# Fifty-one element-wise instructions of a Fourier-mixer encoder layer moved from GpSimd to VectorE

## The chip, the cores and the metric

The kernel runs on one core of a Trainium2 chip. The core has TensorE (PE in the profile, matmuls), VectorE (DVE), ScalarE (ACT), GpSimd (POOL) and SyncE (SP, whose queue issues most of the transfers here). The metric is the time of one execution on the device in microseconds, as a median over runs. Less is better.

## The reference

One layer of a bidirectional encoder on x of shape 1024 x 1024 (positions x channels), float32, with a conditioning vector c. Cut to what is computed (only layer 0 runs, since DEPTH is 1):

```python
mod = silu(c) @ ada_w + ada_b
sh1, sc1, g1, sh2, sc2, g2 = split(mod, 6)
h = layer_norm(x) * (1 + sc1) + sh1
y = real(fft2(h in 8 groups of 128 channels, over positions and channels)) @ w_out
x = layer_norm(ALPHA * x + g1 * y) * ln_mix_g + ln_mix_b
h = layer_norm(x) * (1 + sc2) + sh2
u = h @ w_up                                   # 1024 -> 2 x 2816
u = depthwise conv of width 3 over positions(u) + conv_b
y = (gelu(gate) * val) @ w_down                # 2816 -> 1024
x = layer_norm(ALPHA * x + g2 * y) * ln_ffn_g + ln_ffn_b
```

## The kernel before

Nearly all matmuls work on numbers split into two parts of a shorter float format: `split(hi, lo, src)` has ScalarE copy `src` to `hi` and VectorE (or another engine that is named) subtract `hi` from `src` to give `lo`. Each product is then three matmuls, high x high, high x low and low x high (`hl3`, lines 284 to 286). So every operand costs a ScalarE copy and an element-wise subtraction before TensorE can use it.

The stages in order of time are these.

- Norm and folds (to about 54 us). x is normalised in eight row tiles; tiles are paired, and for each half of the channels (c0 = 0 and 512) sums and differences of pairs are formed: `fb` and `bw` (differences, the odd products), `s` (sums, written over x), `fe` (sums and differences of the sums, the even products). `fold_split` forms a fold and splits it; its low parts are `b`, `bhl` and `el`. `c1_split` splits the three DFT tables into `c1h` and `c1l`.
- Odd and even products `po` and `pe` (the DFT over positions), scaled into `uh` and `ul`, then the DFT over channels in `pp` and `pq`, split into `P` and `Q`. Between them lie the matmuls `ada` of the modulation vectors, whose weights `aw` are loaded through few buffers.
- Mixer weights. `w_prep` loads two tiles per group of channels and GpSimd forms their sum and difference `we` and `wa`. After the gate row `g1` is broadcast, each of the eight is multiplied by `g1` (line 358) and split into `wh` and `wl`.
- Output of the mixer, `A` and `B`, over four pairs of row tiles, with residual, norm, modulation and transposes into `h2t`. GpSimd makes the inverse deviation (`pow`) and some normalised tiles `hm`.
- Up projection. `h2t` is split into `Hh` and `Hl` in four groups of positions; the first two tiles j = 0 and 1 of w_up are used plainly (`plain_w`, parts `a`); `comb` forms the position combinations T1 to T4, which are split into TT1 to TT4; from j = 2 on each tile is done with seven products in place of eight, for which GpSimd forms S1 to S4 of the weights (lines 633 to 636).
- Down projection with the second norm, from about 615 us.

`E(name)` gives GpSimd if the name stands in `ON_POOL`, else VectorE. The order of the instructions in each engine's queue is laid down when the program is built: a planner (`TileContext(..., schedule_with_timeline_sim=True)`) goes through them with costs of its own and issues on each engine what it takes to be ready, in the order of the program where several are. So an instruction given to another engine changes the order of others too. On the chip each queue runs in that order.

Of the kernel before, what the change touches and what calls it, by code (L numbers as in the profile page):

```python
# [11 lines left out]
ALU = mybir.AluOpType  # L12
# [10 lines left out]


ON_POOL = frozenset((
    "H0", "H1", "T1", "T2", "T4", "a0", "a1", "c1l0", "c1l1", "c1l2", "fb0_0", "fb0_512", "fb1_0", "fe00_512",
    "lb1_512", "lb2_512", "lb3_512", "le00_0", "le10_512", "s0_512", "s2_0", "s3_512", "ve2",
))

IN_NAMES = (  # L30
# [6 lines left out]
def encoder_layer(ctx: ExitStack, tc: tile.TileContext, I, out: bass.AP):  # L37
    nc = tc.nc
    act, dve, pool, pe, sp = nc.scalar, nc.vector, nc.gpsimd, nc.tensor, nc.sync
# [6 lines left out]
    def slot(i, shape, dt, name):  # L46
        return big.tile([128] + list(shape), dt, tag=f"s{i}", name=name)
# [4 lines left out]
    def split(hi, lo, src, eng=None):  # L52
        act.activation(hi, src, AF.Copy)  # L53
        (eng or dve).tensor_tensor(lo, src, hi, ALU.subtract)  # L54
# [40 lines left out]
    def bank(i, name, shape=(512,)):  # L95
        return ps.tile([128] + list(shape), F32, tag=f"b{i}", name=name)
# [12 lines left out]
    def ada_load(sec, part=0, parts=1):  # L109

        n = 1024 // parts
        abt = cp.tile([128, 256], F32, tag="abt", bufs=2, name=f"abt{sec}_{part}")
        sp.dma_start(abt[:, : n // 4], I["ada_b"][sec] if parts == 1 else I["ada_b2"][sec, part])
        ws = []
        c0 = 1024 * sec + n * part
        for i in range(KT // parts):
            sl = AW[sec]
            w = slot(sl[(i if sec == 4 else n_aw[0]) % len(sl)], [parts, n], F32, f"aw{sec}_{part}_{i}")
            n_aw[0] += 1
            rows = I["ada_w"][128 * parts * i : 128 * parts * (i + 1), c0 : c0 + n]  # L120
            sp.dma_start(w, rows.rearrange("(k p) n -> p k n", p=128))
            ws += [w[:, k, :] for k in range(parts)]
        return abt, ws, n // 4, f"{sec}_{part}"
# [5 lines left out]
    def ada_mm(sec, loaded, col=None, bk=7, plus=0.0, c0=0, kts=range(KT)):  # L129
        abt, ws, q, nm = loaded  # L130
        if kts[0] == 0:
            pms[sec] = bank(bk, f"ada{nm}", (q,))
        pm = pms[sec]
        for kt in kts:
            for g in range(4):
                pe.matmul(pm[32 * g : 32 * g + 32, :], cb[:, kt, :], ws[kt][:, q * g : q * g + q],
                          start=(kt == 0), stop=(kt == KT - 1), tile_position=(0, 32 * g))
        if kts[-1] != KT - 1:
            return
        if col is not None:  # L140
            act.activation(abt[:, :q], pm, AF.Copy)
        else:
            dve.tensor_tensor(abt[:, :q], pm, abt[:, :q], ALU.add)
        mod_r[sec] = abt
        if col is not None:
            nb_ = q // 128
            pt = bank(7, f"adat{nm}", (nb_, 128))
            for b in range(nb_):
                pe.transpose(pt[:, b, :], abt[:, 128 * b : 128 * b + 128], ident)
            dst, src = col.rearrange("p (i b) -> p i b", b=nb_), pt.rearrange("p b (i r) -> p i b r", r=32)[:, :, :, 0]  # L150
            bias = adab[:, sec, c0 : c0 + 4 * nb_].rearrange("p (i b) -> p i b", b=nb_)
            dve.scalar_tensor_tensor(dst, src, plus, bias, ALU.add, ALU.add)

    def row_bcast(sec, dst, get_bank, scale=1.0):
        for h in range(2):
            pb = get_bank(f"bc{sec}_{h}")
            for q in range(2):
                pe.matmul(pb[:, 256 * q : 256 * q + 256], sel[:, 2 * h + q, :], mod_r[sec], start=True, stop=True)
            act.activation(dst[:, 512 * h : 512 * h + 512], pb, AF.Copy, scale=scale)
# [109 lines left out]
    g1 = slot(7, [D], F32, "g1")  # L269
# [13 lines left out]
    def hl3(ps_ap, hi_l, lo_l, hi_r, lo_r, first, last):  # L283
        pe.matmul(ps_ap, hi_l, hi_r, start=first, stop=False)  # L284
        pe.matmul(ps_ap, hi_l, lo_r, start=False, stop=False)  # L285
        pe.matmul(ps_ap, lo_l, hi_r, start=False, stop=last)  # L286
# [5 lines left out]
    def mm_odd(c):  # L292
        c0 = c // 4 * 512
        cs = slice(128 * c - c0, 128 * c - c0 + 128)
        po = obank(f"po{c}")
        for i, t in enumerate((0, 2, 1, 3)):
            if c0 not in bh[t]:
                pe.matmul(po, bw[t][:, cs], stage_c1[t // 2][:, t % 2, :], start=(i == 0), stop=(i == 3))
                continue
            hl3(po, bh[t][c0][:, cs], bl[t][c0][:, cs], c1h[t // 2][:, t % 2, :], c1l[t // 2][:, t % 2, :], i == 0, i == 3)  # L300
        return po

    def mm_even(c):
        cs = slice(128 * c, 128 * c + 128)
        pv = obank(f"pe{c}")
        for q in range(2):
            fs = slice(256 * q, 256 * q + 256)
            for t in range(2):
                hl3(pv[:, fs], eh[q][t][:, cs], el[q][t][:, cs], c1h[2][:, t, fs], c1l[2][:, t, fs], t == 0, t == 1)
        return pv  # L310

    def odd(u):
        return u.rearrange("p (h i r) -> p h i r", h=2, r=2)[:, :, :, 1]

    def even(u):
        return u.rearrange("p (h i r) -> p r h i", h=2, r=4)[:, 0:4:2]
# [4 lines left out]
    for c in range(8):  # L321
        pv = mm_even(c)
        po = pos_.pop(c)
        uh = slot(2 * (c % 3), [1024], F32R, f"uh{c}")
        ul = slot(2 * (c % 3) + 1, [1024], F32R, f"ul{c}")
        po_v = po.rearrange("p (h i) -> p h i", h=2)
        pv_v = pv.rearrange("p (q h i) -> p q h i", q=2, h=2)
        sc = sc1[:, c : c + 1]
        act.activation(odd(uh), po_v, AF.Identity, scale=sc)
        dve.scalar_tensor_tensor(odd(ul), po_v, sc, odd(uh), ALU.mult, ALU.subtract)  # L330
        last_u = act.activation(even(uh), pv_v, AF.Identity, scale=sc)
        dve.scalar_tensor_tensor(even(ul), pv_v, sc, even(uh), ALU.mult, ALU.subtract)
        dve.tensor_scalar(dcs[:, c, :], pv[:, 0:256:128], sc, None, ALU.mult)
        uv[c] = (uh, ul)
        if c + LOOK < 8:
            pos_[c + LOOK] = mm_odd(c + LOOK)
        for k, u in enumerate((uh, ul)):
            pe.matmul(pN, nyt[:, c, :], u[:, 0:512], start=(c == 0 and k == 0), stop=(c == 7 and k == 1))
        if c % 2 == 0:
            continue  # L340
        gp = c // 2
        pp = bank(4, f"pp{gp}")
        pq = bank(5, f"pq{gp}")
        for dst, base, rng in ((pp, 0, slice(0, 512)), (pq, 256, slice(512, 1024))):
            for e in range(2):
                uh, ul = uv[2 * gp + e]
                ls = slice(base + 128 * e, base + 128 * e + 128)
                hl3(dst, dch_h[:, ls], dch_l[:, ls], uh[:, rng], ul[:, rng], e == 0, e == 1)
        P_t[gp] = slot(36 + gp, [2, 512], F32R, f"P{gp}")
        Q_t[gp] = slot(40 + gp, [2, 512], F32R, f"Q{gp}")  # L350
        split(P_t[gp][:, 0, :], P_t[gp][:, 1, :], pp)
        pool.memset(Q_t[gp][:, :, 0:1].bitcast(F32), 0.0)
        split(Q_t[gp][:, 0, 1:512], Q_t[gp][:, 1, 1:512], pq[:, 1:512])
        if c == 1:
            row_bcast(G1, g1, lambda n: bank(4 + int(n[-1]), n), 1.0 / ALPHA)
            for gp in range(4):
                for w in w_raw[gp]:
                    pool.tensor_tensor(w, w, g1, ALU.mult)
        if c == 1:
            ada_mm(SH1, ada_load(SH1), sh1)  # L360
            shpm = cp.tile([128, 8, 2], F32, name="shpm")
            for k, sgn in ((0, 1.0), (1, -1.0)):
                dve.tensor_scalar(shpm[:, :, k], sh1, sgn * HALF_DC, None, ALU.mult)
        if c == 3:
            sh2 = cp.tile([128, 8], F32, name="sh2")
            ada_mm(SH2, ada_load(SH2), sh2)
        if c == 5:
            sc2 = cp.tile([128, 8], F32, name="sc2")
            ada_mm(SC2, ada_load(SC2), sc2, plus=1.0)
# [201 lines left out]
    a0 = plain_w(0, (45, 44, 31, 32))  # L571
# [30 lines left out]
    a1 = plain_w(1, (33, 24, 25, 26))  # L602
    T1 = comb("T1", B[0, 1], B[0, 0], ALU.subtract, 34)
    T2 = comb("T2", B[1, 1], T1, ALU.subtract, 46)
# [3 lines left out]
    T4 = comb("T4", T2, B[1, 0], ALU.subtract, 31)  # L608
# [317 lines left out]
    for n, (p, i) in enumerate(steps):  # L926
# [51 lines left out]
        for m in range(4):  # L978
            ms = slice(128 * m, 128 * m + 128)
            w = 512 // len(acc[m])  # L980
# [112 lines left out]
```

## Time and profile before

| | |
|---|---|
| time, median of 3 runs | 866.1 us (865.58 to 866.92) |
| the profiled execution's own time | 866.72 us |
| its span, first to last instruction | 864.9 us |
| TensorE busy | 799.9 us, 92% |
| VectorE busy | 708.3 us, 82% |
| ScalarE busy | 387.3 us, 45% |
| GpSimd busy | 328.9 us, 38% |
| mean granted clock of TensorE | 0.974 |

The profile is one execution of the kernel. A busy share is a mean over stages with different limits; which engine waits for which, and when, is read from the views of waits, of stages and of the timeline.

### The profile page before, as it was taken

To read this page: it belongs to the slowest core of one execution; us is meant where nothing else is said; L and a number is where in the kernel's file an instruction comes from. 1 tells how busy PE (TensorE), PEld (TensorE's weight loads), DVE (VectorE), ACT (ScalarE), POOL (GpSimd) and SP (SyncE) were. 2 spreads that over 40 slices of the span, in tenths; PEclk is the share of its full clock that TensorE was granted. 3 is DMA by queue.
4 is the path that set the end of the run, shared out by engine and by line. 5 is a ranking of instruction groups with operands and counts; after the bars stand their busy time and mean duration, and the time that the engine had idled before them with its cause. 6 is when DMAs were issued, how large, how long until landed. Compare 5 with 4: busy or idle time off the path is not lost.

```text
span 864.9 us, 10742 instructions
## 1 busy us (share of the span) xinstructions
PE 799.9 (92%) x3943; PEld 644.2 (74%) x3943; DVE 708.3 (82%) x979; ACT 387.3 (45%) x559; POOL 328.9 (38%) x256
## 2 busy tenths in 40 slices
PE   2699799997979999999999999999999989999990
PEld 1466577776868888888888888888887868888880
DVE  6972857899899999998888888888677784556897
ACT  7442514676454344444444444444444324335611
POOL 5767802498355434334334333431000112702203
PEclk9899899999989999999999999999999999999995
DMA  9759665562113222322212222210498887988903
GB/s 342 260 181 309 248 230 210 186 262 74 49 49 97 98 74 74 111 84 98 74 73 74 87 90 92 98 50 25 156 375 309 264 215 147 190 157 240 294 26 122
DMA packets 50613, 133.90 MB, mean 155 GB/s; under 512 B 5608, under 2 KB 6760, under 8 KB 50560
## 3 DMA queue, kind: packets, MB, share of 16 engines
q1 hardware_dynamic: 39504, 103.59, 34.1%
q0 software_dynamic: 10768, 28.58, 13.4%
q10 hardware_dynamic: 288, 1.05, 0.3%
q8 instruction: 31, 0.51, 0.2%
q14 instruction: 22, 0.18, 0.1%
HBM read 110.39 MB, written 19.92 MB: 151 GB/s over the span
## 4 chain that ended last, share of the span: by engine, by line
PE 57%; DVE 6%; DMA 6%; issue 2%; POOL 1%; ACT 1%; SPq 0%; POOLq 0%; ACTq 0%; DVEq 0%
PE x L286 14%; PE x L284 14%; PE x L285 14%; PE o L285 5%; PE o L286 5%; PE o L284 5%; DMA gr<-gd 2%; DMA xu<-x1d 2%; DMA wd<-in_w_down_dram 1%; DVE d_1l L54 1%; DVE d_0l L54 1%; DMA Sg<-gd 1%; DVE C L864 1%; POOL S L635 0%; DVE C L894 0%
## 5 line engine op out<-in xcount | busy, mean ns | idle before, releaser
L285 PE MATMUL x<-Hl,a 128*128 128x512 f32 (+2 forms) x416 | 156.7, 378 | 4.8 <-DVE Hl L54 4.0
L284 PE MATMUL x<-Hh,a 128*128 128x512 f32 (+2 forms) x416 | 155.6, 377 | 4.6 <-ACT a L53 4.6
L286 PE MATMUL x<-Hh,a 128*128 128x512 f32 (+2 forms) x416 | 155.9, 375 | 0.0
L285 PE MATMUL o<-d_1l,d_0h 128*128 128x512 f32 (+1 forms) x299 | 115.0, 386 | 4.0 <-DVE d_1l L54 4.0
L286 PE MATMUL o<-d_1h,d_0l 128*128 128x512 f32 (+1 forms) x299 | 114.4, 384 | 0.0
L284 PE MATMUL o<-d_1h,d_0h 128*128 128x512 f32 (+1 forms) x299 | 102.8, 383 | 0.0
L285 PEld LDWEIGHTS x<-Hl,a 128*128 128x128 f32 x416 | 79.0, 190 | 20.2 <-DVE Hl L54 5.1
L284 PEld LDWEIGHTS x<-Hh,a 128*128 128x128 f32 x416 | 78.5, 190 | 20.8 <-ACT a L53 5.5
L53 ACT ACTIVATE a<-S 128x512 fp32r<-128x512 f32 x80 | 50.4, 630 | 96.2 <-PE x L286 87.9
L286 PEld LDWEIGHTS x<-Hh,a 128*128 128x128 f32 x416 | 79.0, 190 | 14.6 <-POOL nbm L478 0.4
L588 POOL DMA_DIRECT2D gd<-ug x20 | 11.4, 568 | 170.2 <-DVE ug L587 170.2
L285 PEld LDWEIGHTS o<-d_1l,d_0h 128*128 128x128 f32 x299 | 56.8, 190 | 16.5 <-DVE d_1l L54 5.3
L54 DVE TENSOR_TENSOR a<-wu,a 128x512 fp32r<-128x512 f32 x60 | 63.5, 1059 | 3.0 <-ACT a L53 3.0
L286 PEld LDWEIGHTS o<-d_1h,d_0l 128*128 128x128 f32 x299 | 56.6, 189 | 10.9
L284 PEld LDWEIGHTS o<-d_1h,d_0h 128*128 128x128 f32 x299 | 56.2, 188 | 11.0
L54 DVE TENSOR_TENSOR a<-S,a 128x512 fp32r<-128x512 f32 x80 | 60.9, 762 | 0.8
L635 POOL TENSOR_TENSOR S<-wu 128x512 f32<-128x512 f32 x20 | 29.9, 1493 | 69.1 <-DVE a L54 60.4
L53 ACT ACTIVATE a<-wu 128x512 fp32r<-128x512 f32 x60 | 37.5, 626 | 40.5 <-PE x L286 38.6
L733 POOL DMA_DIRECT2D Sg<-gd x12 | 14.7, 1266 | 89.3 <-DVE d_0l L54 89.3
L579 DVE SCALAR_TENSOR_TENSOR t<-uv,cw,t 128x1023 f32<-128x1023 f32 x20 | 35.9, 1793 | 11.4 <-ACT t L578 11.3
L54 DVE TENSOR_TENSOR d_1l<-wd,d_1h 128x1024 fp32r<-128x1024 f32 (+1 forms) x37 | 44.0, 1189 | 0.0
L636 POOL TENSOR_TENSOR S<-wu,S 128x512 f32<-128x512 f32 x20 | 43.9, 2195 | 0.1
(325 smaller groups left out, 1929.7 us busy)
## 6 DMA issues: line engine op xcount, KB each, us to landing
aw<-in_ada_w_dram SPq DMA_DIRECT2D x48, 512.0 KB, 6.0
wu<-in_w_up_dram SPq DMA_DIRECT2D x44, 512.0 KB, 3.2
gd<-ug POOLq DMA_DIRECT2D x20, 512.0 KB, 2.9
wd<-in_w_down_dram SPq DMA_DIRECT2D x20, 512.0 KB, 9.7
gr<-gd SPq DMA_DIRECT2D x15, 512.0 KB, 7.4
gA<-gd SPq DMA_DIRECT2D x10, 512.0 KB, 10.7
Sg<-gd POOLq DMA_DIRECT2D x10, 512.0 KB, 6.5
x<-in_x_dram SPq DMA_DIRECT2D x8, 512.0 KB, 5.4
```

What stands on the lines that cost most here:

```text
L53: act.activation(hi, src, AF.Copy)
L54: (eng or dve).tensor_tensor(lo, src, hi, ALU.subtract)
L284: pe.matmul(ps_ap, hi_l, hi_r, start=first, stop=False)
L285: pe.matmul(ps_ap, hi_l, lo_r, start=False, stop=False)
L286: pe.matmul(ps_ap, lo_l, hi_r, start=False, stop=last)
L579: dve.scalar_tensor_tensor(tt[:, 1:S], u[:, 0 : S - 1], w[:, 0:1], tt[:, 1:S], ALU.mult, ALU.add)
L588: pool.dma_start(gd[j], gg)
L635: pool.tensor_tensor(S3, A11, A21, ALU.subtract)
L636: pool.tensor_tensor(S4, A12, S2, ALU.subtract)
L733: pool.dma_start(raw_g[p, i] if p == 7 else Sg[i], gd[k0 : k0 + n, :, 512 * mh : 512 * mh + 512].rearrange("k p c -> p k c"), accum_op=ALU ...
L864: dve.scalar_tensor_tensor(c1[:, lo], c1[:, lo], rs, ffb[:, lo], ALU.mult, ALU.add)
```

## The change

The names in `ON_POOL` are taken out, all but `ve2`, and the eight gate products are given to VectorE. Moved from GpSimd to VectorE are thus: three low parts `c1l` (128x1024); twelve folds, sums and low parts of folds (128x512); eight gate products (128x1024); the low parts of groups 0 and 1 of the up projection's input for every second tile, eight of 128x256; the low parts of the first two up tiles, eight of 128x512; the combinations T1, T2 and T4, twelve of 128x512. That is 51 instructions. GpSimd keeps `pow`, `nbm`, `hm`, the sums and differences `we` and `wa`, S1 to S4, its memsets and its transfers.

```diff
 ON_POOL = frozenset((
-    "H0", "H1", "T1", "T2", "T4", "a0", "a1", "c1l0", "c1l1", "c1l2", "fb0_0", "fb0_512", "fb1_0", "fe00_512",
-    "lb1_512", "lb2_512", "lb3_512", "le00_0", "le10_512", "s0_512", "s2_0", "s3_512", "ve2",
+    "ve2",
 ))
@@
             for gp in range(4):
                 for w in w_raw[gp]:
-                    pool.tensor_tensor(w, w, g1, ALU.mult)
+                    dve.tensor_tensor(w, w, g1, ALU.mult)
```

## Rows read from the trace of the kernel before

**Rows 1.** The first part of the page: the span, and for each engine its busy microseconds, share of the span and instructions.
```profile
span 864.9 us, 10742 instructions
...
PE 799.9 (92%) x3943; PEld 644.2 (74%) x3943; DVE 708.3 (82%) x979; ACT 387.3 (45%) x559; POOL 328.9 (38%) x256
```

**Rows 2.** The table of stages: start and end of the stretch and its length in us, then for each engine its busy us and the number of its instructions, the granted clock of TensorE (1.00 is full speed), the mean busy share of the DMA engines, and GB/s.
```profile
15.00:45.00 30.00, 20.85 (x156) 12.65 (x156) 29.16 (x34) 15.39 (x24) 22.86 (x14) 0.89 0.80 282
...
60.00:95.00 35.00, 35.00 (x260) 23.66 (x260) 15.11 (x19) 15.53 (x21) 28.53 (x14) 1.00 0.86 290
...
172.00:200.00 28.00, 24.77 (x211) 19.20 (x209) 26.13 (x65) 20.63 (x52) 25.03 (x26) 1.00 0.63 236
200.00:230.00 30.00, 27.09 (x151) 23.64 (x152) 30.00 (x33) 15.12 (x34) 21.25 (x14) 0.94 0.10 36
...
265.00:615.00 350.00, 350.00 (x1546) 289.97 (x1545) 315.97 (x394) 152.78 (x205) 126.81 (x90) 1.00 0.22 80
```

**Rows 3.** The view of the waits of TensorE up to 270 us: line and tile of the waiting matmul, what it waited for, and the total in us, the number of times and the longest.
```profile
PE po L286 <- DVE b L54: 5.6, 1, 5.6
PE x L284 <- ACT a L53: 4.6, 2, 2.5
PE B L285 <- DVE wl L54: 4.6, 2, 2.3
PE x L285 <- DVE Hl L54: 4.0, 4, 1.8
PE pe L286 <- DVE el L54: 1.3, 1, 1.3
PE po L284 <- DVE ul L330: 1.1, 1, 1.1
```

**Rows 4.** The same table as rows 2 for short stretches.
```profile
80.00:90.00 10.00, 10.00 (x73) 5.90 (x73) 4.02 (x7) 4.79 (x7) 10.00 (x5) 1.00 0.91 311
30.00:35.00 5.00, 1.18 (x3) 0.99 (x4) 4.97 (x7) 2.06 (x4) 2.81 (x2) 0.63 1.03 403
35.00:40.00 5.00, 4.39 (x16) 3.34 (x14) 5.00 (x5) 2.66 (x8) 3.69 (x3) 0.69 0.13 42
100.00:105.00 5.00, 3.24 (x8) 2.56 (x9) 5.00 (x8) 2.07 (x2) 4.00 (x3) 0.50 0.49 190
210.00:215.00 5.00, 3.21 (x15) 2.98 (x15) 5.00 (x6) 2.87 (x8) 5.00 (x4) 0.72 0.18 70
```

**Rows 5.** The timeline of VectorE around 25 to 31 us: start and duration in us, engine, line, operation, output and inputs by the names of the program, shapes, and count.
```profile
25.63 1.77 DVE L54 TENSOR_TENSOR el<-fe,eh 128x512 fp32r<-128x512 f32 x1
...
30.20 0.69 DVE L246 TENSOR_TENSOR x<-x,x 128x512 f32<-128x512 f32 x1
30.81 0.68 DVE L198 TENSOR_TENSOR fb<-x,x 128x512 f32<-128x512 f32 x1
```

**Rows 6.** The timeline of GpSimd in the same stretch, columns as before.
```profile
25.12 1.73 POOL L54 TENSOR_TENSOR el<-fe,eh 128x512 fp32r<-128x512 f32 x1
```

**Rows 7.** The timeline of VectorE at three instructions that give prices: a 128x1024 product, a 128x256 subtraction, and the instruction behind it.
```profile
116.60 1.22 DVE L388 TENSOR_TENSOR wnr<-wnr,g 128x1024 f32<-128x1024 f32 x1 [3.49 <-DMA wnr<-in_w_ny_dram]
...
172.30 0.41 DVE L54 TENSOR_TENSOR Hl<-h2t,Hh 128x256 fp32r<-128x256 f32 x1
172.63 0.68 DVE L455 SCALAR_TENSOR_TENSOR s<-B,xr 128x512 f32<-128x512 f32 x1
```

**Rows 8.** The groups of VectorE instructions from 14.6 to 54 us, one line of the kernel and one shape to a group: busy us in total and mean ns of one, then the idle time before them.
```profile
L198 DVE TENSOR_TENSOR fe<-x,x 128x512 f32<-128x512 f32 x7 | 10.2, 1497 | 0.0
L246 DVE TENSOR_TENSOR x<-x,x 128x512 f32<-128x512 f32 x5 | 6.6, 1335 | 0.1
L54 DVE TENSOR_TENSOR el<-fe,eh 128x512 fp32r<-128x512 f32 x6 | 6.2, 1040 | 0.0
L198 DVE TENSOR_TENSOR fb<-x,x 128x512 f32<-128x512 f32 x4 | 5.8, 1462 | 0.0
...
L54 DVE TENSOR_TENSOR bhl<-fb,bhl 128x512 fp32r<-128x512 f32 x1 | 1.8, 1772 | 0.0
```

**Rows 9.** The timeline of GpSimd over the gate products, first and last of eight (the last line holds two).
```profile
81.17 2.38 POOL L358 TENSOR_TENSOR we<-we,g 128x1024 f32<-128x1024 f32 x1
...
97.27 6.69 POOL L358 TENSOR_TENSOR wa<-wa,g 128x1024 f32<-128x1024 f32 x2
```

**Rows 10.** The timeline of ScalarE where the gate row g1 is written.
```profile
77.55 0.60 ACT L159 ACTIVATE g<-bc 128x512 f32<-128x512 f32 x1 [0.27 <-PE bc L158]
```

**Rows 11.** The groups of VectorE instructions from 78 to 112 us, columns as in rows 8.
```profile
L54 DVE TENSOR_TENSOR wl<-wa,wh 128x1024 fp32r<-128x1024 f32 x4 | 9.1, 2312 | 0.0
L54 DVE TENSOR_TENSOR wl<-we,wh 128x1024 fp32r<-128x1024 f32 x4 | 7.5, 1916 | 2.5 <-ACT wh L53 2.5
```

**Rows 12.** The groups of VectorE instructions from 168 to 227 us, columns as in rows 8.
```profile
L54 DVE TENSOR_TENSOR Hl<-h2t,Hh 128x256 fp32r<-128x256 f32 x16 | 9.3, 610 | 0.0
L54 DVE TENSOR_TENSOR Hl<-h2t,Hh 128x258 fp32r<-128x258 f32 x8 | 9.1, 1173 | 0.0
...
L54 DVE TENSOR_TENSOR TT1l<-T,TT1h 128x512 fp32r<-128x512 f32 x4 | 6.0, 1500 | 0.0
L54 DVE TENSOR_TENSOR TT2l<-T,TT2h 128x512 fp32r<-128x512 f32 x4 | 4.8, 1225 | 0.0
...
L537 DVE TENSOR_TENSOR T<-h2t,h2t 128x512 f32<-128x512 f32 x4 | 4.8, 1229 | 0.0
```

## Prediction

> **What bounds the kernel now.** I read the page first: TensorE (PE) is busy 92% of the 864.9 us span [rows 1]. That is a mean over stages, so the next view is the table of stages [rows 2]. From 265 to 615 us PE is busy all 350 us; nothing that the change touches lies there, and what is gained in front of it only moves it. From 60 to 95 us PE is also never idle. It is idle from 15 to 45 us (20.9 of 30 us busy) and from 172 to 230 us (24.8 of 28, 27.1 of 30). The view of PE's waits names the causes [rows 3]: 5.6, 1.3 and 1.1 us for low parts b, el and ul that VectorE (DVE) writes in the stage of the odd and even products; 4.6 us for wl, the low parts of the mixer weights; 4.0 us for Hl, the low parts of the up projection's input; 4.6 us for a, a high part written by ScalarE.
>
> After three of these waits PE runs slower as well. In 30 to 40, 100 to 105 and 210 to 215 us the mean granted clock is 0.50 to 0.72, a mix of the two levels 1.2 and 2.4 GHz [rows 4]. Busy time times the missing share of the clock is what that costs: 1.18 x 0.37 + 4.39 x 0.31 = 1.8 us, 3.24 x 0.50 = 1.6 us, and 3.21 x 0.28 = 0.9 us.
>
> DVE feeds PE in these stages, and DVE is full there: 29.2 of 30 us from 15 to 45 us, 26.1 of 28 and 30.0 of 30 us from 172 to 230 us [rows 2]. What is in those busy microseconds decides the case.
>
> **What a DVE instruction costs beside GpSimd.** An addition or subtraction of two 128x512 tiles in SBUF takes DVE 0.68 or 0.69 us, 0.61 us from start to start, at 30.2 and 30.8 us; the same kind of instruction takes 1.77 us at 25.6 us [rows 5], beside a GpSimd subtraction of 1.73 us that runs from 25.1 to 26.9 us [rows 6]. DVE ends about when GpSimd's turn and its own 0.6 us are over. So the two engines do such work in turns, and GpSimd's turn is the longer one. The Trainium skill, page "SBUF — State Buffer", section "SBUF: two separate sides", says that the port pair which VectorE and GpSimd share is an exclusive lock held for a whole instruction, not a split bandwidth; the trace agrees (1.77 us beside GpSimd, 0.68 us alone).
>
> **The change, stage by stage.** No instruction disappears: 51 leave GpSimd's queue and stand in DVE's. Price on DVE: 0.60 us for 128x512 (start to start, above); 1.20 us for 128x1024 (1.22 us for the product wnr) and 0.33 us for 128x256 (0.41 us, the next one starting 0.33 us later) [rows 7].
>
> *Stage A, folds, 14.6 to 54 us.* Added: three c1l of 1024 and twelve pieces of 512: 3 x 1.20 + 12 x 0.60 = 10.8 us. Given back: fe, x, el, fb and bhl on DVE are 7 + 5 + 6 + 4 + 1 = 23 instructions with 10.2 + 6.6 + 6.2 + 5.8 + 1.8 = 30.6 us; alone they would take 23 x 0.68 = 15.6 us, so 15.0 us is waiting for GpSimd [rows 8]. Net on DVE: 10.8 - 15.0 = -4.2 us. DVE is the feeder here, so PE's waits of 5.6 + 1.3 + 1.1 = 8.0 us shrink by 4.2 us. What is behind, 60 to 95 us, is PE's own work and moves forward whole. I leave the 1.8 us of half clock as it is, since some wait remains. Bounds: nothing gained (DVE's order puts the three c1l in front of the folds that PE wants first), to all of 8.0 + 1.8 = 9.8 us.
>
> *Stage B, gate products, 78 to 112 us.* The eight products w = w x g1 run on GpSimd one behind the other from 81.2 to 104.0 us, 22.8 us [rows 9], though g1 is ready when ScalarE ends it at 78.2 us [rows 10]. Splitting w waits for them, and PE waits for wl. On DVE they cost 8 x 1.20 = 9.6 us. The eight wl, now 7.5 + 9.1 = 16.6 us [rows 11], fall to 8 x 1.22 = 9.8 us, so 6.8 us comes back. Net on DVE +2.8 us, and here that is free: from 80 to 90 us DVE is busy 4.0 of 10 us [rows 4]. The products of groups 0 and 1 (four), their four wl and those 4.0 us take 4.8 + 4.8 + 4.0 = 13.6 us from 78.2 us, which ends at 91.8 us, in front of the 95 us up to which PE has work without a gap [rows 2]. So the 4.6 us of waiting for wl go, and I count half of the 1.6 us of clock: 5.4 us. Bounds: 2 us (one wait stays, because products of groups 2 and 3 stand in front of the first wl), to 4.6 + 1.6 = 6.2 us.
>
> *Stage C, end of the norm and first up tiles, 168 to 227 us.* Added: eight a of 512, eight Hl of 256, twelve T of 512: 4.8 + 2.6 + 7.2 = 14.6 us. Given back: 24 Hl take 18.4 us and would take 24 x 0.41 = 9.8 us; DVE's four TT1l, four TT2l and four T take 15.6 us and would take 12 x 0.68 = 8.2 us; together 16.0 us [rows 12]. Net -1.4 us, which I take off the 4.0 us of waits for Hl. GpSimd's own steps of the norm also lose their neighbours, which I price at nothing: DVE's queue is full either way. Bounds: 4 us lost (T pieces of 7.2 us in front of the last Hl group, some 3 us of it hidden by work that PE has in hand), to 4.0 + 0.9 = 4.9 us gained.
>
> *After it.* The 4.6 us wait for a stays: it hangs on S, the GpSimd additions of the first planned tile, which are not moved.
>
> Sum: 4.2 + 5.4 + 1.4 = 11.0 us. The profiled execution took 866.7 us (span 864.9 and 1.8 outside), 0.6 us above the median of the runs, 866.1. From the median: 855.
>
> **Rivals.**
> 1. *DMA paces the middle.* The DMA engines are 0.86 busy from 60 to 95 us [rows 2]. If G1's weights and w_ab arrive no earlier, stage A's gain is lost there and B and C remain: 866.1 - 5.4 - 1.4 = 859. Against it: from 35 to 40 us the share is 0.13 [rows 4], so there those loads wait for something other than bandwidth, and the buffers that they wait for come free earlier.
> 2. *DVE becomes the bound: slower.* DVE gets 10.8 + 9.6 + 14.6 = 35.0 us more and must regain 15.0 + 6.8 + 16.0 = 37.8 us. In stage B its idle time covers the difference; in A and C what counts is 25.4 us added against a share r of 31.0 us regained. With B's 5.4 us the sum is zero at r = 0.65; below that the kernel is slower. At r = 0.3 it is 25.4 - 9.3 - 5.4 = +10.7 us, 877. For it: DVE is at its limit in A and C, one queue in order has to do what two did, and the norm's short steps then stand behind long pieces. Against it: the instructions that meet no GpSimd work take 0.68 us, so r should be near 1. The Trainium skill, page "Perfetto Trace Analysis", section "Optimizing Scalar/DVE Operations", advises handing work from a saturated DVE to other engines, GpSimd even, which speaks against this change; it adds that the shared port may spoil that, and [rows 5, 6] side with the addition.
> 3. *Everything goes through.* All waits of A, B and C with their clock: 9.8 + 6.2 + 4.9 = 20.9 us, 845.
> 4. *No change.* The engines' lists are ordered anew by the planner, and a new wait of some 10 us in A or C takes the place of what is won: 866.
>
> **How the numbers follow.** My forecast, 848 to 861 with its bounds partly met, 0.48; DMA paces (856 to 863) 0.18; everything goes through 0.10; no change 0.08; slower 0.16. A measurement of this kernel tells 0.2%, 1.7 us, from no change. Faster: 0.48 + 0.18 + 0.10 = 0.76; same 0.08; slower 0.16. A range of 845 to 867 leaves out nearly all of rival 2 and half of rival 3, about 0.2.
>
> **What would show it.** In the new trace: DVE's 128x512 pieces at 0.68 us all through 15 to 54 us; the wait for b below 3 us; no wait for wl; gate products at 1.2 us each, ended by 92 us; Hl near 0.41 us; and the stretch in which PE is never idle, from 265 us on, starting some 11 us earlier. Wrong, if the DVE pieces stay long without GpSimd beside them, if PE's waits for po and pe grow beyond 8 us, or if an order in which DVE does T pieces ahead of Hl opens a wait of several us near 210 us.

## The result: 1.3% faster, and the profile after

| | before | after |
|---|---|---|
| time, median | 865.9 us (865.58 to 866.92) | 855.7 us (853.01 to 858.2) |
| ratio | | 0.987 (95% interval 0.9845 to 0.9894) |
| the profiled execution's own time | 866.72 us | 853.01 us |

855 was forecast, 855.7 measured. (The ratio is estimated over all runs and gives 11.3 us; the two medians differ by 10.2 us.) The number is right; how it came about is not what the sum said. By the runs below, term A was less than half of what A gave, term B nearly twice what B gave or more, and C is two large effects that nearly cancel.

The head of the page of after, to be read against [rows 1]:

```profile
span 851.1 us, 10735 instructions
...
PE 797.7 (94%) x3943; PEld 643.7 (76%) x3943; DVE 702.5 (83%) x1030; ACT 387.0 (45%) x559; POOL 244.5 (29%) x205
```

VectorE took over 51 instructions and is busy 5.8 us less than before (702.5 against 708.3 us). GpSimd lost 84 us.

The table of stages of after, columns as in [rows 2], and below it one stretch of before that rows 2 do not hold:

```profile
15.00:45.00 30.00, 27.18 (x201) 15.99 (x202) 29.42 (x57) 19.91 (x32) 4.80 (x4) 0.94 0.94 339
...
35.00:40.00 5.00, 4.58 (x49) 3.25 (x50) 5.00 (x10) 2.53 (x5) 0.00 (x0) 1.00 0.91 344
...
60.00:95.00 35.00, 35.00 (x246) 25.39 (x245) 30.89 (x37) 18.81 (x23) 8.83 (x6) 1.00 0.82 289
95.00:125.00 30.00, 30.00 (x196) 20.56 (x195) 20.72 (x49) 8.48 (x21) 3.43 (x3) 1.00 0.64 233
...
172.00:200.00 28.00, 19.75 (x148) 17.77 (x148) 20.82 (x59) 16.40 (x40) 8.91 (x10) 0.86 0.28 94
...
265.00:615.00 350.00, 350.00 (x1546) 289.88 (x1545) 313.56 (x391) 150.88 (x202) 120.91 (x88) 1.00 0.23 85
```

```profile
95.00:125.00 30.00, 25.42 (x153) 18.05 (x152) 21.83 (x36) 10.09 (x19) 10.91 (x6) 0.89 0.73 253
```

Three readings. From 15 to 45 us VectorE does 57 instructions where it did 34 in the same busy time, and PE is busy 6.3 us more. From 95 to 125 us PE was idle 4.6 us at a granted clock of 0.89; now it has no gap and the full clock. From 172 to 200 us PE is worse off: 19.75 of 28 us busy at 0.86, against 24.77 at 1.00 [rows 2].

The waits of PE in after up to 270 us, to be read against [rows 3]:

```profile
...
PE x L283 <- ACT Hh L52: 4.2, 3, 3.0
PE trm L486 <- POOL hm L479: 3.1, 1, 3.1
PE ada L135 <- DMA aw<-in_ada_w_dram: 1.8, 1, 1.8
PE x L284 <- DVE Hl L53: 1.8, 3, 1.1
PE po L283 <- ACT b L52: 1.0, 1, 1.0
PE x L285 <- DVE a L53: 0.9, 1, 0.9
```

The waits for b, el and wl are gone. So is the 4.6 us wait for a, which was to stay. In their place stand Hh (three waits) and hm, both in the part where the norm meets the up projection.

The prices held. The groups of VectorE from 14.6 to 54 us in after, against [rows 8]:

```profile
L53 DVE TENSOR_TENSOR el<-fe,eh 128x512 fp32r<-128x512 f32 x8 | 5.4, 680 | 0.0
L245 DVE TENSOR_TENSOR x<-x,x 128x512 f32<-128x512 f32 x8 | 5.3, 675 | 0.0
L197 DVE TENSOR_TENSOR fe<-x,x 128x512 f32<-128x512 f32 x8 | 5.2, 680 | 0.0
L197 DVE TENSOR_TENSOR fb<-x,x 128x512 f32<-128x512 f32 x6 | 4.0, 683 | 0.0
```

All are at 0.68 us, where they were at 1.04 to 1.50. The gate products in VectorE's timeline (start, duration), against [rows 9]:

```profile
64.60 2.61 DVE L357 TENSOR_TENSOR we<-we,g 128x1024 f32<-128x1024 f32 x1 [2.48 <-ACT g L158]
67.13 3.42 DVE L357 TENSOR_TENSOR wa<-wa,g 128x1024 f32<-128x1024 f32 x1
70.48 1.21 DVE L357 TENSOR_TENSOR we<-we,g 128x1024 f32<-128x1024 f32 x1
...
76.16 1.21 DVE L357 TENSOR_TENSOR wa<-wa,g 128x1024 f32<-128x1024 f32 x1
```

Six take 1.21 us as priced. The first two take 2.61 and 3.42 us beside the last of the sums `we` and `wa` that stayed on GpSimd. All are done at 77.4 us, 15 us ahead of what was called for, because g1 itself is ready at 64.5 us and not at 78.2 us [rows 10]. The low parts Hl of 128x256 in after, 150 to 227 us, against [rows 12]:

```profile
L53 DVE TENSOR_TENSOR Hl<-h2t,Hh 128x256 fp32r<-128x256 f32 x24 | 9.6, 429 | 0.0
```

### The profile page after: what moved, and what is told of

Its sections match the earlier page's. It is cut to its first block, busy times and chain, and to the rows that moved or that the text cites. A ratio compares the mean times of both kernels' runs of the same rounds, so it can differ in the third digit from the quotient of the medians.

```text
span 851.1 us, 10735 instructions
## 1 busy us (share of the span) xinstructions
PE 797.7 (94%) x3943; PEld 643.7 (76%) x3943; DVE 702.5 (83%) x1030; ACT 387.0 (45%) x559; POOL 244.5 (29%) x205
## 4 chain that ended last, share of the span: by engine, by line
PE 74%; DVE 11%; DMA 9%; issue 3%; ACT 2%; POOL 1%; SPq 0%; POOLq 0%; DVEq 0%; ACTq 0%
PE x L284 16%; PE x L285 16%; PE x L283 16%; PE o L284 4%; PE o L285 4%; PE o L283 4%; DMA xu<-x1d 4%; PE ada L135 2%; DMA gr<-gd 2%; DMA wd<-in_w_down_dram 1%; PE B L283 1%; DVE d_1l L53 1%; PE B L285 1%; PE B L284 1%; DVE d_0l L53 1%
## 5 line engine op out<-in xcount | busy, mean ns | idle before, releaser
L283 PEld LDWEIGHTS x<-Hh,a 128*128 128x128 f32 x416 | 79.9, 193 | 19.6 <-ACT Hh L52 5.1
L285 PEld LDWEIGHTS x<-Hh,a 128*128 128x128 f32 x416 | 79.4, 191 | 15.1 <-DVE a L53 1.3
L285 PEld LDWEIGHTS o<-d_1h,d_0l 128*128 128x128 f32 x299 | 56.7, 189 | 10.9
L587 POOL DMA_DIRECT2D gd<-ug x20 | 11.5, 573 | 170.4 <-DVE ug L586 170.4
L634 POOL TENSOR_TENSOR S<-wu 128x512 f32<-128x512 f32 x20 | 28.1, 1406 | 63.1 <-DVE a L53 57.2
L578 DVE SCALAR_TENSOR_TENSOR t<-uv,cw,t 128x1023 f32<-128x1023 f32 x20 | 34.6, 1731 | 11.6 <-ACT t L577 11.5
L52 ACT ACTIVATE d_0h<-Sg 128x1024 fp32r<-128x1024 f32 x15 | 15.9, 1061 | 56.6 <-PE o L284 56.6
```

What stands on the lines that cost most here:

```text
L578: dve.scalar_tensor_tensor(tt[:, 1:S], u[:, 0 : S - 1], w[:, 0:1], tt[:, 1:S], ALU.mult, ALU.add)
L587: pool.dma_start(gd[j], gg)
L634: pool.tensor_tensor(S3, A11, A21, ALU.subtract)
```

## The experiments

All runs, by their ratio to the kernel before on the same chip. "Against before" is (ratio - 1) x 866.1 us, with the ratio of all runs and not that of the two medians, so that runs of different chips can be compared. A stands for the folds and c1l, B for the gate products, C for the rest (H, a, T).

| kernel | on VectorE | median us | ratio (95%) | against before, us |
|---|---|---|---|---|
| after | A, B, C | 855.7 | 0.987 (0.9845 to 0.9894) | -11.3 |
| a_only | A | 858.3 | 0.9888 (0.9856 to 0.992) | -9.7 |
| b_only | B | 865.2 | 0.9983 (0.9968 to 0.9999) | -1.5 |
| c_only | C | 867.2 | 1.0004 (0.9993 to 1.0014) | +0.3 |
| ab | A, B | 854.3 | 0.9853 (0.9831 to 0.9874) | -12.7 |
| ab_plus_tt | A, B; 15 extra GpSimd additions | 873.6 | 1.0066 (1.0046 to 1.0086) | +5.7 |
| ab_plus_set | A, B; 18 extra fills | 865.6 | 0.997 (0.9957 to 0.9982) | -2.6 |
| ab_add | A, B; 12 additions, clean | 865.4 | 0.9972 (0.9956 to 0.9988) | -2.4 |
| ab_set | A, B; 12 fills, clean | 854.0 | 0.9835 (0.9806 to 0.9864) | -14.3 |
| ab_t | A, B, T | 845.5 | 0.9737 (0.9722 to 0.9751) | -22.8 |
| ab_ha | A, B, H, a | 864.5 | 0.9956 (0.9941 to 0.9971) | -3.8 |
| ab_t_h | A, B, T, H | 844.4 | 0.974 (0.9698 to 0.9782) | -22.5 |
| ab_t_a | A, B, T, a | 851.3 | 0.9809 (0.9784 to 0.9834) | -16.5 |

### Each part alone

The diffs of this group are against the kernel after.

**a_only.** The names of C are left in `ON_POOL`, and the gate products stay on GpSimd:

```diff
 ON_POOL = frozenset((
+    "H0", "H1", "T1", "T2", "T4", "a0", "a1",
     "ve2",
@@
-                    dve.tensor_tensor(w, w, g1, ALU.mult)
+                    pool.tensor_tensor(w, w, g1, ALU.mult)
```

> Only stage A moves to VectorE: the three c1l and the twelve folds, sums and low parts. My sum: 4.2 us faster, 862 from 866. The reading of the changed kernel's trace (its last even product ends 5.5 us earlier and its last mixer product 14.7 us earlier): 5 to 6 us faster, 860. Rival 2 (VectorE as the bound): slower than before by up to 10.8 us. In the trace VectorE's 128x512 pieces should stand at 0.68 us up to 54 us.

Measured: -9.7 us. The last even product ends 5.4 us earlier than before (90.59 against 95.99 us), near the 4.2 us of the sum. But the last mixer product ends 12.8 us earlier (159.42 against 172.24), though the gate products did not move to another engine. They still run on GpSimd at 2.4 us each, only from 67.1 to 90.5 us in place of 81.2 to 104.0 [rows 9]. The stage in which PE used to wait for wl, in a_only:

```profile
95.00:125.00 30.00, 30.00 (x200) 20.01 (x199) 23.11 (x51) 7.74 (x20) 3.46 (x3) 1.00 0.70 252
```

No gap, full clock. So A alone removes nearly all that the prediction booked under B: of the 4.6 us of waiting for wl 1.0 us is left, ahead of 95 us. Why the gate products start earlier is read from the DMA share: from 35 to 40 us it was 0.13 [rows 4], and is 0.91 in after and 1.02 in a_only. Of the eight loads of the weights `aw` for G1 the last four are issued from 60.7 us on before and from 44.4 us on in after, and the broadcast of g1 starts 13.6 us earlier (61.98 against 75.62 us). By the trace these loads wait for PE: their buffers come free as PE does the modulation products `ada`, of which those for G1 start at 60.0 us before and at 43.7 us in after. They stand in PE's queue among the products that wait for the folds, so folds that end sooner bring these loads forward too. This is read from the traces; no run moves the loads alone.

**b_only.** The reverse: the names of A and C in `ON_POOL`, the gate products on VectorE.

```diff
-    "ve2",
+    "H0", "H1", "T1", "T2", "T4", "a0", "a1", "c1l0", "c1l1", "c1l2", "fb0_0", "fb0_512", "fb1_0", "fe00_512",
+    "lb1_512", "lb2_512", "lb3_512", "le00_0", "le10_512", "s0_512", "s2_0", "s3_512", "ve2",
```

> Only stage B moves: the eight gate products. My sum: 5.4 us faster, 861, with the wait for wl gone. The reading of the changed trace, by which stages A and B give 14.7 us together and A some 5.5 of them: 9 us faster, 857. Rival: the gate products stand in the way of ul, P and Q and a new wait takes the place of that for wl: no change, 866.

Measured: -1.5 us. VectorE's timeline in b_only around the gate products:

```profile
78.38 2.00 DVE L360 TENSOR_TENSOR we<-we,g 128x1024 f32<-128x1024 f32 x1 [3.76 <-ACT g L161]
...
90.44 0.68 DVE L56 TENSOR_TENSOR P<-pp,P 128x512 fp32r<-128x512 f32 x1
```

With g1 as late as before, the eight products occupy VectorE from 78.4 to 90.4 us, and P, Q and the ul of the DFT over channels stand behind them. PE's last even product comes 5.2 us later. The wait for wl is gone and the last mixer product ends 4.5 us earlier; in the profiled execution 3.0 us of that are left at the end, over all runs 1.5 us. The rival that was written down beforehand, that the products stand in the way of ul, P and Q, describes this best.

**c_only.** C taken out of `ON_POOL`, A and the gate products as before.

```diff
-    "ve2",
+    "c1l0", "c1l1", "c1l2", "fb0_0", "fb0_512", "fb1_0", "fe00_512",
+    "lb1_512", "lb2_512", "lb3_512", "le00_0", "le10_512", "s0_512", "s2_0", "s3_512", "ve2",
@@
-                    dve.tensor_tensor(w, w, g1, ALU.mult)
+                    pool.tensor_tensor(w, w, g1, ALU.mult)
```

> Only stage C moves: a, Hl of two groups, T1, T2, T4. My sum: 1.4 us faster, 865. The reading of the changed trace, where TensorE is 15.1 us ahead at the first up product and 10.1 us ahead at the third stored tile: 4 to 5 us slower, 870. If the loss there comes only from what stages A and B bring forward, no change, 866.

Measured: +0.3 us, within noise. It is not that C does nothing. The stage behind 230 us, before and then in c_only:

```profile
230.00:265.00 35.00, 30.36 (x124) 24.29 (x123) 30.27 (x34) 19.99 (x31) 16.91 (x10) 0.90 0.22 70
```

```profile
230.00:265.00 35.00, 34.04 (x149) 27.56 (x148) 29.58 (x34) 19.96 (x32) 14.36 (x9) 1.00 0.17 60
```

Here PE gains 3.7 us of idle time and the clock; from 160 to 230 us it loses 3.3 us of busy time (60.55 against 63.86 us) and some clock. Two opposite effects cancel, and the third group takes them apart.

**ab.** A and B on VectorE, C left on GpSimd.

```diff
 ON_POOL = frozenset((
+    "H0", "H1", "T1", "T2", "T4", "a0", "a1",
     "ve2",
```

> Stages A and B move, stage C stays with GpSimd. My sum: 9.6 us faster, 856.5, so 1.4 us slower than the changed kernel. The reading of the changed trace: 14 to 15 us faster, 851, that is 4 us faster than the changed kernel. If the three parts are not additive because the planner orders the lists anew each time, it differs from the sum of the runs of A and B alone by more than 3 us.

Measured: -12.7 us. That is as fast as the whole change, within the intervals: C as a whole earns nothing on top. And B on top of A earns 3.0 us, not 5.4; the intervals of ab and a_only overlap, so that it earns anything is not shown.

### Is it GpSimd's reading of SBUF?

**ab_plus_tt and ab_plus_set.** To ab, GpSimd work is given back that nobody needs: its output `scr` is read by no one. In the first it is 15 additions that read x tiles and the DFT tables, in the second 18 fills, each batch held back by a two-column addition.

```diff
+    def extra(src, n=512):
+        pool.tensor_tensor(scr[:, :n], src, src, ALU.add)      # ab_plus_tt
+        # ab_plus_set: tensor_tensor on 2 columns, then n // 512 times memset(scr, 0.0)
@@ behind each c1 split, each fold_split of b and each pair of fold_splits of e
+            extra(...)
```

> Stages A and B on VectorE as in the run ab, and beside stage A fifteen extra GpSimd additions of the old sizes (twelve 128x512, three 128x1024) that read SBUF and whose output nobody uses. Turn-taking: each stops one VectorE piece for a GpSimd turn, 1.1 us at 512 and 2.2 us at 1024, together some 19 us at most; VectorE's pieces stand at 1.8 us and more again, the last even product ends 10 us or more later than in ab, and the kernel takes 864 us or more against 854. Rival (the gain of stage A is the shorter latency of the pieces and another order, and GpSimd's presence costs nothing): 854.

> As the run before, but the fifteen extra GpSimd pieces are memsets of about the same length (128x1024 each, eighteen in all), each behind an addition of two columns that holds it at its place. If GpSimd stops VectorE only when it reads SBUF: VectorE's pieces stay at 0.68 us and the kernel at 854 us. If any GpSimd work on SBUF does it: pieces of 1.6 us and 860 us or more.

Measured: 18.4 and 10.1 us slower than ab. The additions make VectorE's pieces long again (x 1.13, fe 1.08 us) and the fills do not (0.68 to 0.69 us), but the fills cost 10 us all the same. ScalarE's timeline in ab_plus_set names a fault of the experiment:

```profile
42.98 0.72 ACT L339 ACTIVATE uh<-po,sc 128x512 fp32r<-128x512 f32 x1 [4.51 <-POOL scr L204]
```

`uh` is written into the buffers of x, and the extra additions read x late, so ScalarE waited for them. Neither run prices the reading.

**ab_add and ab_set.** The same without that fault: twelve additions of 512 columns that read only the DFT tables, or twelve fills of 1024 columns, behind one two-column addition that holds them until the last row pair's norm. The order of the instructions on all the other engines is the same as in ab.

```diff
+    def extra(src):
+        pool.tensor_tensor(scr[:, :512], src, src, ALU.add)    # ab_add
+        # ab_set: pool.memset(scr, 0.0)
@@
+    pool.tensor_tensor(scr[:, 0:2], nb, nb, ALU.add)
     c1_split()
@@ behind each fold_split of b and each pair of fold_splits of e
+            extra(stage_c1[...][:, ..., :])
```

> Stages A and B on VectorE, C on GpSimd, and on GpSimd, behind the last row pair's 128x2 power, twelve additions of 512 columns that read the first-column tables (whose buffers nothing claims before 90 us) into a buffer that nobody reads. VectorE's, TensorE's and ScalarE's orders are those of the kernel with A and B. If a GpSimd operation that reads SBUF stops VectorE: the pieces behind about 26 us go from 0.68 to about 1.1 us, the last even first product comes 4 to 8 us later, and the time is 858 to 862. If the earlier test with additions was slow only because ScalarE waited for the buffers they read: 854 and pieces of 0.68 us.

> The same with twelve fills of 1024 columns (0.95 us each) in place of the additions, which read nothing in SBUF. If only reading stops VectorE: pieces stay at 0.68 us, and the time is that of A and B alone, 853 to 856. If any work on GpSimd stops it: pieces near 1 us for the 11 us that the fills last, and 856 to 859.

Measured: the fills cost nothing (854.0 us); the additions cost 11.9 us (-2.4 against -14.3). The timeline of GpSimd, then of VectorE, in ab_add:

```profile
26.76 17.27 POOL L204 TENSOR_TENSOR scr<-c1raw 128x512 f32<-128x512 f32 x12
```

```profile
32.94 1.52 DVE L198 TENSOR_TENSOR fb<-x,x 128x512 f32<-128x512 f32 x1
34.38 1.52 DVE L54 TENSOR_TENSOR bhl<-fb,bhl 128x512 fp32r<-128x512 f32 x1
```

The same stretch in ab_set, GpSimd first:

```profile
27.37 12.08 POOL L204 MEMSET scr<- 128x1024 f32 x12
```

```profile
30.19 0.69 DVE L198 TENSOR_TENSOR fb<-x,x 128x512 f32<-128x512 f32 x1
30.79 0.68 DVE L54 TENSOR_TENSOR bhl<-fb,bhl 128x512 fp32r<-128x512 f32 x1
```

Beside additions VectorE's pieces start 1.44 us apart, one piece to one addition (17.27 / 12 = 1.44); beside fills 0.60 us apart. The pieces take 1.52 us where about 1.1 was expected. Twelve times 0.84 us is 10.1 us. The last even product ends 10.2 us later than in ab (101.13 against 90.90 us), and the time is 11.9 us longer than with fills, 10.3 us longer than in ab. So a GpSimd addition of SBUF tiles delays VectorE by a whole turn, a GpSimd fill does not, and in this stage all of that delay reaches the end. This shows the cause of A's gain in its own stage; that A gives more than it gains there hangs on the earlier g1, as read above.

The Trainium skill, page "SBUF — State Buffer", section "SBUF: two separate sides", limits the lock, for a VectorE operation with two SBUF inputs, to the case "only against a GpSimd op that reads SBUF"; 1.44 us beside additions and 0.60 us beside fills agree with it.

### What C consists of

**ab_t and ab_ha.** From ab, T1, T2 and T4 go to VectorE, or H and a do.

```diff
 ON_POOL = frozenset((
-    "H0", "H1", "T1", "T2", "T4", "a0", "a1",
+    "H0", "H1", "a0", "a1",                 # ab_t
+    "T1", "T2", "T4",                       # ab_ha
```

> Stages A and B on VectorE, and of stage C only T1, T2 and T4; Hl of groups 0 and 1 and a stay with GpSimd. If stage C loses because Hl and a stand in front of the norm's short steps in VectorE's queue (the last normalised tile's transposes end at 196.8 us in the changed kernel and at 191.8 us in ab): as fast as ab or up to 3 us faster, 852 to 854. If the T pieces do it: 857 to 859.

> Stages A and B on VectorE, and of stage C only Hl of groups 0 and 1 and a; T1, T2 and T4 stay with GpSimd. If Hl and a delay the norm's short steps: the transposes end near 196 us and the kernel takes 857 to 859. If the T pieces are what costs: 853 to 854.

Measured: T gains 10.1 us (-22.8 against -12.7), H and a lose 8.9 us (-3.8 against -12.7). Both times lie outside all that was expected of them. C's zero is the sum of two large numbers. Where T's gain lies is shown by the stage table, first of ab, then of ab_t:

```profile
230.00:265.00 35.00, 30.43 (x125) 24.45 (x124) 35.00 (x35) 14.74 (x22) 23.36 (x13) 0.90 0.28 91
```

```profile
190.00:230.00 40.00, 37.60 (x198) 31.63 (x197) 37.67 (x57) 27.84 (x52) 12.88 (x7) 1.00 0.11 40
230.00:265.00 35.00, 34.86 (x152) 28.43 (x153) 34.88 (x36) 13.13 (x20) 18.00 (x12) 1.00 0.27 91
```

In ab PE loses 4.57 us of idle time and 30.43 x 0.10 = 3.0 us of clock from 230 to 265 us; in ab_t 0.1 us. The idle time is two waits for a, high parts of the first planned tile: one of 2.19 us for a part that ScalarE makes straight from the weights at 231.75 us, behind other late work of its queue, and one of 2.4 us for a part made from S. GpSimd's timeline of ab up to the first S, then that of ab_t:

```profile
205.27 6.61 POOL L537 TENSOR_TENSOR T<-T,h2t 128x512 f32<-128x512 f32 x4 [2.41 <-PE x L286]
221.61 0.63 POOL L588 DMA_DIRECT2D gd<-u  x1 [9.72 <-DVE u L587]
230.95 3.97 POOL L635 TENSOR_TENSOR S<-wu 128x512 f32<-128x512 f32 x1 [8.71 <-ACT u L616]
```

```profile
220.36 3.15 POOL L633 TENSOR_TENSOR S<-wu,wu 128x512 f32<-128x512 f32 x1 [26.24 <-DMA wu<-in_w_up_dram]
```

In ab_t S starts 10.6 us earlier, as soon as the weights are there. In ab T holds GpSimd until 211.9 us (and VectorE beside it: two TT2l take 3.48 us at 207.3 us), but that is not what S waits for. S1 to S4 are written into the buffers of T4 (31 and 32 in the kernel), and these come free when ScalarE and VectorE have split T4 into TT4. ScalarE and VectorE at the first split in ab, then ScalarE in ab_t:

```profile
222.87 1.14 ACT L53 ACTIVATE TT4h<-T 128x512 fp32r<-128x512 f32 x2
```

```profile
229.51 1.29 DVE L54 TENSOR_TENSOR TT4l<-T,TT4h 128x512 fp32r<-128x512 f32 x2
```

```profile
213.07 0.62 ACT L53 ACTIVATE TT4h<-T 128x512 fp32r<-128x512 f32 x1
```

In ab S starts 0.15 us behind the end of these TT4l, and so it does before and in b_only. T4 is complete at about 212 us in both, but in ab_t ScalarE takes up its first piece 9.8 us earlier. So the gain of T came, as far as these rows show, through the order of a queue that nobody edited; no run tests that order alone. GpSimd's timeline of after names the same wait:

```profile
233.17 1.53 POOL L634 TENSOR_TENSOR S<-wu 128x512 f32<-128x512 f32 x1 [5.85 <-ACT u L615]
237.12 1.67 POOL L632 TENSOR_TENSOR S<-wu,wu 128x512 f32<-128x512 f32 x1 [2.42 <-DVE TT4l L53]
```

In after S is even later than in ab, and PE's wait is gone all the same, because PE comes later too: its first matmul behind the 288 of the two plain tiles starts at 230.78 us, against 224.40 us in ab. Measured from that matmul, the first S starts 5.8 to 8.9 us later in the five kernels with T on GpSimd (before, a_only, b_only, ab, ab_ha), and from 2.9 us earlier to 2.9 us later in the five with T on VectorE (after, c_only, ab_t, ab_t_h, ab_t_a).

**ab_t_h and ab_t_a.** On top of ab_t, only H or only a.

```diff
-    "H0", "H1", "a0", "a1",
+    "a0", "a1",                             # ab_t_h
+    "H0", "H1",                             # ab_t_a
```

> A, B and the combinations T on VectorE, and of the rest of C only the low parts of the first two thirds of the activations (H0, H1); a stays on GpSimd. If the low parts on VectorE are what gives the ten microseconds back (they stand in its queue among the norm steps of the last row pairs): about 854. If it is the Winograd combinations a: about 845.5.

> The same with only the combinations a on VectorE and the low parts on GpSimd. If it is a: 853 to 855, the power of the second row pair's norm 5 us later, as in the changed kernel. If it is the low parts: about 845.5, and that power stays near 171 us. If each costs a part, both kernels lie near 850.

Measured: H costs +0.3 us (the interval is 3.6 us to either side: one execution, the profiled one, took 851.1 us, the others 843.5 to 844.8), a costs 6.3 us, and both together, which is after, 11.5 us. PE's idle time from 160 to 230 us, and its busy time times the missing share of the clock there, by the stage tables of these kernels:

| kernel | idle, us | clock, us | sum | against ab_t | time against ab_t |
|---|---|---|---|---|---|
| ab_t | 4.8 | 1.7 | 6.5 | | |
| ab_t_h | 5.1 | 1.5 | 6.7 | +0.2 | +0.3 |
| ab_t_a | 7.9 | 4.2 | 12.2 | +5.7 | +6.3 |
| after | 10.1 | 7.3 | 17.4 | +10.9 | +11.5 |

The two rows of after behind the last line; that of ab_t for 190 to 230 us stands above:

```profile
160.00:190.00 30.00, 23.36 (x182) 19.50 (x183) 25.49 (x76) 19.96 (x49) 10.00 (x11) 0.86 0.54 202
190.00:230.00 40.00, 36.54 (x191) 31.54 (x191) 31.03 (x57) 22.52 (x46) 2.57 (x4) 0.89 0.14 53
```

So the loss lies there, though a count from one execution each is good only to some 3 us: GpSimd issues the transfer of the twentieth product tile at 577.02 us in ab_t, and 2.9, 5.7 and 8.0 us later in ab_t_h, ab_t_a and after (the trace of ab_t_h is that of its slowest execution). VectorE is not full there: 25.5 of 30 and 31.0 of 40 us. What is late is one chain, the norm of the second pair of rows, which goes through VectorE several times. Its steps in VectorE's timeline of ab_t, then of after:

```profile
163.13 1.74 DVE L469 SCALAR_TENSOR_TENSOR s<-s,rs_m,mixb 128x1024 f32<-128x1024 f32 x1 [0.64 <-POOL rs_m L426]
...
170.94 0.14 DVE L424 TENSOR_SCALAR ve_hm<-stm 128x1 f32<-128x1 f32 x1
```

```profile
164.91 0.41 DVE L499 TENSOR_SCALAR h2t<-trm,sc,sh 128x128 f32<-128x128 f32 x1 [1.60 <-PE trm L486]
...
165.89 1.27 DVE L468 SCALAR_TENSOR_TENSOR s<-s,rs_m,mixb 128x1024 f32<-128x1024 f32 x1
...
173.75 0.42 DVE L142 TENSOR_TENSOR abt<-ada,abt 128x256 f32<-128x256 f32 x1 [1.32 <-PE ada L135]
...
175.75 0.14 DVE L423 TENSOR_SCALAR ve_hm<-stm 128x1 f32<-128x1 f32 x1
```

In ab_t VectorE waits 0.64 us for GpSimd's rs_m and starts the first step when it is there. In after rs_m is there no later (162.93 against 163.10 us), but the step starts 2.8 us later, behind Hl and h2t, of which one h2t waits 1.60 us for a transpose `trm` by PE. PE's timeline of after, then of ab_t, at the first of these transposes:

```profile
161.44 1.08 PE L135 MATMUL ada<-aw,cb 128*32 128x256 f32 x8 [1.84 <-DMA aw<-in_ada_w_dram]
...
163.90 1.41 PE L486 MATMUL trm<-ident,hm 128*128 128x128 f32 x8
```

```profile
161.13 0.66 PE L487 MATMUL trm<-ident,hm 128*128 128x128 f32 x4
```

In after PE has modulation products `ada` in front of them and waits 1.84 us for their weights. Counted from the end of the last mixer product, these transposes start after 6.4 us in after, 6.5 us in ab_ha and 7.4 us in ab_t_a, the kernels of A and B with a on VectorE, and after 2.9 to 3.2 us in ab, ab_t and ab_t_h. The step `ve_hm` in turn stands behind `abt`, which waits 1.32 us for PE's `ada`, and comes 4.8 us later. Steps of 0.14 us wait in a queue that is idle in between, for what stands in front of them. So two queues take part, VectorE's and PE's, and the planner ordered both anew when a was moved. No run changes an order alone: that the order makes the loss is read from these rows and not tested, and how it divides between the two queues stays open. That a and H together cost some 5 us more than each by itself is no more than the intervals allow, and the traces (2.9, 5.7 and 8.0 us) do not show it.

## Why the prediction came out right, point by point

**What bounds the kernel**: right. The stages that were named are those that moved, and 265 to 615 us stayed at 350 us busy.

**The price on VectorE**: right. 0.68, 1.21 and 0.43 us were found where 0.68, 1.22 and 0.41 were called, and VectorE's busy time fell, to 702.5 us where the three nets give 705.5. That the engines take turns is shown by ab_add and ab_set. The count was uneven in one point: what is added was priced from start to start (0.60 us), what stays at its full duration (0.68 us). With 0.60 us for both, A's net on VectorE is -6.0 us, near the 5.5 us by which the last even product came earlier.

**Stage A, -4.2 us**: too small. The last even product came 5.5 us earlier in after; in its own stage the term is near. But alone A gives 9.7 us, since G1's loads, and with them g1, come earlier too. Rival 1's counter-argument had seen this (the DMA share of 0.13, loads that wait for buffers and not for bandwidth), and the sum did not use it: it moved "what is behind" forward by 4.2 us and left g1 at 78.2 us.

**Stage B, -5.4 us**: the effect came, and for another reason. The step that failed is the start at 78.2 us: with g1 at 64.5 us GpSimd's own eight products are nearly in time (a_only waits 1.0 us for wl). B alone gives 1.5 us, because from 78 to 90 us VectorE was not free for it: its idle time there (4.0 of 10 us busy [rows 4]) was time ahead of P and ul, which b_only pushes back. From the start to the end of the last mixer product A and B were to give 9.6 us; they gave 14.7 (172.24 to 157.55 us).

**Stage C, -1.4 us**: near in the net, and by luck. Busy time was counted (added 14.6, regained 16.0), and by VectorE's total that count was near. The step that failed is to take the net of busy time for the gain. What decided, as far as the rows above show, was order: T on VectorE takes 10.1 us off the time, H and a put 11.5 us back. Against ab the whole of C costs 1.4 us, within the intervals. In the traces after is 14.7 us ahead at the last mixer product and 12.6 us at the transfer of the twentieth product tile (585.03 against 597.64 us), a loss of some 2 us. That is inside the bounds (4 us lost to 4.9 us gained), which hold neither of its two parts.

**"The 4.6 us wait for a stays"**: failed. It is gone where T has left GpSimd (ab keeps T there and has the wait, ab_t has not). The step looked at S, which was not moved, and not at what S itself waits for, the split of T4, whose buffers it takes.

So the sum of -11 met -11.3 by compensation: A and B gave 12.7 us together where 9.6 were called (3.1 too little), and C cost 1.4 us where a gain of 1.4 was called (2.8 too much). Of the rivals, DMA did not pace the middle (share 0.82 from 60 to 95 us, PE without a gap). Rival 2 named part of what took the gain of C back ("the norm's short steps then stand behind long pieces"), but made it hang on a share r of regained busy time. The pieces are all short, r is near 1, and the steps are late even so. Of the signs, waits at po and pe did not grow, but one of 3.1 us for hm and three for Hh, 4.2 us together, opened where PE had waited for Hl. And PE's last gap ahead of the long stretch ends 7.2 us earlier (241.62 against 248.78 us), not 11.

The best version found is ab_t: A, B and T on VectorE, H and a on GpSimd, 845.5 us, 23 us below the kernel before and some 11 below the changed one. ab_t_h cannot be told from it.

## What to carry to other kernels

Price a move between two engines twice: by busy time, which here came out within 3 us of 700, and by what stands behind what in each queue that is changed, which by these rows made 10 us either way at a busy share that hardly moved. When a feeding stage ends earlier, follow what comes free with it to the next loads before booking a later stage's wait to that stage's own edit. And split a move of many pieces by kind before accepting or dropping it: a part that measures as nothing may be two large parts of opposite sign.

## What was not expected of the hardware

A GpSimd fill of 128x1024 takes 0.95 us and leaves VectorE's 128x512 pieces at 0.60 us from start to start; an addition of 128x512 stretches them to 1.44 us. After PE's waits near 160 to 200 us the mean granted clock of TensorE, a mix of the levels 1.2 and 2.4 GHz, was 0.86 from 160 to 190 us and 0.89 from 190 to 230 us in after; that costs 7.3 us beside 10.1 us of idle time, so each microsecond of waiting there cost some 1.7.
